# A new searched order, the first h earlier, and one last store in a two-layer decoder trunk

## The chip, the cores and the metric

The kernel runs on one core of one Trainium2 chip. The time is the device time of one execution in microseconds, and the figure compared is the median over several runs. Beside it there is one profiled execution, whose trace says what each engine did.

The engines have these names: PE is TensorE (matrix multiplies), PEld its weight loads, DVE is VectorE, ACT is ScalarE, POOL is GpSimd, and SP is SyncE, which in this kernel issues nearly all DMA transfers. A line number such as L126 is the line of the kernel that recorded an instruction.

## The reference

The program computes a hybrid decoder trunk of two layers on x (256 positions, width 2048) and a conditioning vector c (width 2048), all in float32:

```python
for layer in range(2):
    shift, scale, gate = split(silu(c) @ ada_w[layer] + ada_b[layer], 3)    # ada_w: 2048 x 6144
    h = x * (1.0 + scale) + shift
    if layer == 0:
        y = ssd_mixer(h, ...)        # h @ a_in_w (2048 x 10304), causal conv, state-space scan, gate, @ a_out_w (4096 x 2048)
    else:
        y = dilated_mixer(h, ...)    # h @ b_in_w (2048 x 4096), three dilated attention groups, gate, @ b_out_w (1024 x 2048)
    x = layer_norm(alpha * x + (1.0 + gate) * y, ln_g[layer], ln_b[layer])
    if layer == 0:
        k_sh, v_sh = shared_kv(x, kv_w)      # x @ kv_w (2048 x 6144)
return x
```

Most of the work is the large matrix products, each of whose weights is read from memory once, and the two `silu(c) @ ada_w` products, which read 50 MB each for a single vector.

## The kernel before, in words

**Products in two parts.** A float32 weight is split into a high part that TensorE takes at its fast rate and a low part that holds the rest. `load_piece` (L115) reads a weight piece `raw` of 128 x 1024 numbers (512 KB) with a DMA on the SP queue. `split` (L122) lets ACT copy it to `whi` (L126) and DVE subtract that from `raw` to get `wlo` (L127). There are 393 such splits. The activation h is split in the same way into a high part (`hhi`, in the traces `act`) and a low part (`hlo`). PE then makes three products, high by high, low by high and high by low, and adds them in one accumulator. L161 to L164 (`cm_piece`), L175 and L177 (`cm_part`) and L216 to L218 are these products. At the start the first four pieces are loaded and split in two halves each (128 x 512), and those halves are the first work of PE.

**The columns of ada_w.** `silu(c)` is spread over all partitions by `spread` (L516: PE makes the copy in an accumulator, ACT copies it to `cb__72`, L522). Then DVE multiplies a loaded block `araw` (128 x 2048, 1 MB) with it and sums along the row: L298 in `ada_dot`. One such dot gives 128 entries of shift, scale or gate. For the first two tiles of 128 entries the dot is cut in smaller pieces (L303), since h cannot be made without them.

**The first h.** The width of 2048 is 16 tiles of 128. `h_step` (L452) makes one of them. Its shift and scale are the sums of L308 and L309. For tile 0, ACT makes the high part in one step straight from x (L471), and DVE makes the plain product `htmp` (L472), from which the low part is subtracted later. For all the others ACT makes the plain product `htmp` (L468) and copies it to the high part (L469).

**What sets the order.** The program is written as one list of instructions. `arrange` (L1630) then searches an order: `forward` (L1330) simulates each engine with a table of durations and a model of DMA, and each trial moves some keys in a stretch of 100 us at random. ROUNDS trials are made, and the order with the smallest simulated end is the one that is built. In the model a DMA adds its bytes divided by RATE (425 GB/s) to the time at which DMA is free (L1392). Each engine runs its own list strictly in the order found, SP included, so that an instruction that waits holds up everything behind it on the same engine. Pairs in `PINS` (L613 to L623 for the start) fix the order of two instructions beforehand.

**The last store.** The output goes out in blocks. The last block of 128 rows is finished by `by_root` (L1104): a product on PE, a copy on ACT (L1107) and a store (L1108). Columns 1024 to 1536 are done in two halves of 256 columns, one stored on the ACT queue and the other on SP behind the store of L1123.

## Time and profile before

| what | value |
|---|---|
| runs | 1243.59, 1243.82, 1248.12 us, median 1243.82 |
| the profiled execution | 1245.2 us, span of its trace 1243.3 us |
| PE busy | 1229.1 us (99% of the span) |
| DVE busy | 1033.1 us (83%) |
| ACT busy | 702.9 us (57%) |
| DMA | 334.46 MB, mean 269 GB/s, up to 422 GB/s in a slice |
| weight splits (L126, L127) | 393 each |
| dots over a whole column block (L298) | 92, 2286 ns each |

A row of the grouped views and of the timeline is read so: start and length in us (in the timeline), engine, line, operation, output and inputs by the program's names, partitions x elements, and the count; in brackets stands the idle time of the engine just before, and what ended it. "PE acc L177 <- DVE wlo L127: 2.2, 3, 1.7" in the list of waits says that PE waited 2.2 us in all, 3 times, at most 1.7 us, for a low weight part of DVE. In the table by stretch an engine's entry is its busy time with the number of its instructions; behind POOL stand the granted clock of TensorE (1.00 is full speed), the busy share of the DMA engines and GB/s.

### The profile page before, as it was taken

The numbers are of one execution on the slowest core, as the hardware profiler recorded it, in microseconds if no ns is written. First come the engines' busy times: TensorE is split into PE (matmuls) and PEld (weight loads), VectorE is DVE, ScalarE is ACT, GpSimd is POOL, SyncE is SP. The second block draws the span as 40 slices with busy tenths as digits, with TensorE's granted clock in tenths as the row PEclk, the third lists the DMA queues.
The fourth block names the chain that finished last, engine by engine and source line by source line (L and its number), as shares of the span: only waits on it lengthen the run. The fifth ranks groups of instructions, "written<-read, shape, count | busy, mean of one in ns | idle before, by whom it ended". The sixth has DMA issues, their size and how long they took to land.

```text
span 1243.3 us, 18078 instructions
## 1 busy us (share of the span) xinstructions
PE 1229.1 (99%) x6712; PEld 1059.3 (85%) x6712; DVE 1033.1 (83%) x1480; ACT 702.9 (57%) x1055; POOL 0.2 (0%) x4
## 2 busy tenths in 40 slices
PE   8999999999999999999999999999999999999998
PEld 7989888888888888888888888888888888888886
DVE  5999998989999999968987698999945746757777
ACT  4645476668848589864345455444445644444561
POOL 0000000000000000000000000000000000000000
PEclk9999999999999999999999999999999999999999
DMA  9999977755786855648997679999965553452571
GB/s 368 421 422 422 422 266 236 249 200 193 265 311 236 308 195 192 240 159 321 395 390 258 234 249 370 393 393 400 374 226 184 196 186 116 158 192 75 192 282 68
DMA packets 81886, 334.46 MB, mean 269 GB/s; under 512 B 9124, under 2 KB 10116, under 8 KB 69640
## 3 DMA queue, kind: packets, MB, share of 16 engines
q1 hardware_dynamic: 81656, 333.20, 72.9%
q8 instruction: 52, 0.85, 0.3%
q14 instruction: 34, 0.28, 0.1%
q10 hardware_dynamic: 144, 0.13, 0.0%
HBM read 331.11 MB, written 2.18 MB: 268 GB/s over the span
## 4 chain that ended last, share of the span: by engine, by line
PE 91%; DMA 3%; DVE 3%; issue 1%; ACT 0%; SPq 0%; DVEq 0%
PE acc L175 24%; PE acc L216 13%; PE acc L217 13%; PE acc L218 13%; PE acc L177 13%; PE acc L163 2%; PE acc L161 2%; PE acc L164 2%; PE py L725 2%; DMA raw<-in_win 2%; DMA araw<-in_ada 2%; DVE wlo L127 1%; DVE araw L298 1%; PE po L1013 1%; PE aux L989 1%
## 5 line engine op out<-in xcount | busy, mean ns | idle before, releaser
L126 ACT ACTIVATE whi<-raw 128x1024 fp32r<-128x1024 f32 (+1 forms) x393 | 408.9, 1048 | 321.1 <-PE acc L175 130.9
L127 DVE TENSOR_TENSOR wlo<-raw,whi 128x1024 fp32r<-128x1024 f32 (+1 forms) x393 | 469.9, 1210 | 114.4 <-ACT whi L126 109.1
L175 PE MATMUL acc<-act,whi 128*128 128x512 f32 x1456 | 379.9, 395 | 0.6 <-DVE kk L198 0.6
L175 PEld LDWEIGHTS acc<-act,whi 128*128 128x128 f32 x1456 | 261.4, 188 | 46.3 <-issue 0.9
L217 PE MATMUL acc<-wlo,act 128*128 128x512 f32 x672 | 257.0, 394 | 0.0
L216 PE MATMUL acc<-whi,act 128*128 128x512 f32 x672 | 252.6, 396 | 0.1
L298 DVE SCALAR_TENSOR_TENSOR araw<-araw,cb__72 128x2048 f32<-128x2048 f32 x92 | 210.1, 2286 | 15.3 <-DMA araw<-in_ada 15.2
L177 PEld LDWEIGHTS acc<-act,wlo 128*128 128x128 f32 x1456 | 201.3, 190 | 17.6 <-DVE wlo L127 3.3
L177 PE MATMUL acc<-act,wlo 128*128 128x256 f32 x1456 | 213.2, 284 | 2.3 <-DVE wlo L127 2.2
L218 PE MATMUL acc<-whi,act 128*128 128x512 f32 x432 | 161.1, 393 | 0.0
L217 PEld LDWEIGHTS acc<-wlo,act 128*128 128x128 f32 x672 | 126.6, 188 | 26.1 <-issue 0.7
L216 PEld LDWEIGHTS acc<-whi,act 128*128 128x128 f32 x672 | 126.0, 188 | 26.0 <-issue 0.7
L218 PEld LDWEIGHTS acc<-whi,act 128*128 128x128 f32 x432 | 81.1, 188 | 16.6 <-issue 0.5
L218 PE MATMUL acc<-whi,ylo 128*128 128x512 f32 x240 | 89.8, 391 | 0.0
L163 PE MATMUL acc<-act,whi 128*128 128x256 f32 x208 | 52.3, 285 | 3.2 <-ACT act L469 2.1
L164 PE MATMUL acc<-act,wlo 128*128 128x256 f32 x208 | 52.8, 285 | 0.0
L218 PEld LDWEIGHTS acc<-whi,ylo 128*128 128x128 f32 x240 | 44.9, 188 | 9.2 <-DVE ylo L785 0.2
L163 PEld LDWEIGHTS acc<-act,whi 128*128 128x128 f32 x208 | 38.5, 192 | 4.5 <-ACT act L469 2.3
L161 PE MATMUL acc<-act,whi 128*128 128x256 f32 x208 | 42.1, 285 | 0.0
L683 ACT ACTIVATE seg<-cbc,cumT 128x128 f32<-128x128 f32 x128 | 40.1, 389 | 0.6 <-DMA cbc<-cumd 0.6
L164 PEld LDWEIGHTS acc<-act,wlo 128*128 128x128 f32 x208 | 38.8, 193 | 0.7
L383 DVE SCALAR_TENSOR_TENSOR cacc<-ct,prm,cacc 128x255 f32<-128x255 f32 (+2 forms) x84 | 37.0, 475 | 1.0 <-ACT cacc L380 0.8
(270 smaller groups left out, 1152.5 us busy)
## 6 DMA issues: line engine op xcount, KB each, us to landing
araw<-in_ada SPq DMA_DIRECT2D x92, 1024.0 KB, 7.5
raw<-in_win SPq DMA_DIRECT2D x86, 512.0 KB, 9.9
raw<-in_wsub SPq DMA_DIRECT2D x70, 512.0 KB, 4.2
raw<-in_wout SPq DMA_DIRECT2D x64, 512.0 KB, 5.4
raw<-in_wbin SPq DMA_DIRECT2D x64, 512.0 KB, 3.9
raw<-in_wkv SPq DMA_DIRECT2D x48, 512.0 KB, 4.3
raw<-in_wk SPq DMA_DIRECT2D x48, 512.0 KB, 6.8
cbc<-cumd SPq DMA_DIRECT2D x16, 512.0 KB, 5.3
```

Of the source, the lines that this page charges most:

```text
L126: S.activation(hi[:, c_], raw[:, c_], AF.Copy)
L127: m = V.tensor_tensor(lo[:, c_], raw[:, c_], hi[:, c_].bitcast(F32), op=ALU.subtract)
L161: T.matmul(o, hi[:, k, c_], alo[:, kt, :], start=False, stop=kt == k1 - 1, skip_group_check=True)
L163: note("product", T.matmul(o, hi[:, k, c_], ahi[:, kt, :], start=kt == k0 and n % 2 == 0, stop=False, skip_group_check=True))
L164: T.matmul(o, lo[:, k, c_], ahi[:, kt, :], start=False, stop=False, skip_group_check=True)
L175: T.matmul(ps[n], hi[:, k, c_], both[:, kt], start=first, stop=False, skip_group_check=True)
L177: T.matmul(ps[n][:, 0, :], lo[:, k, c_], high[:, kt, :], start=first, stop=False, skip_group_check=True)
L216: begin = T.matmul(ps[b], h_, hi[:, k, :], start=kt == k0, stop=False)
L217: T.matmul(ps[b], h_, lo[:, k, :], start=False, stop=False)
L218: end = T.matmul(ps[b], l_, hi[:, k, :], start=False, stop=kt == k1 - 1)
L298: V.scalar_tensor_tensor(raw, raw, 1.0, cb_, op0=ALU.mult, op1=ALU.mult, accum_out=to)
L683: m = S.activation(seg[:, hh, b, :], cbc[:, hh, b, :], AF.Relu, bias=cumT[:, b, h0 + hh:h0 + hh + 1], scale=-1.0)
```

## The change

It has three parts.

- **The first two h.** Tile 1 is now made like tile 0: its high part in one ACT step from x, and its plain product on DVE. New pins put the first high h behind the copy of the first half of the first weight piece and ahead of that of the second piece's first half, and the second high h behind the first piece's second half and ahead of the second piece's second half; the later copies of the spread c come behind the first high h.
- **The last store.** The two halves of columns 1024 to 1536 go out in one store of 256 KB on SP, behind the store of the last 512 columns.
- **The search.** In its model no DMA lands before 3.5 us (FIRST) plus its own time, and past 155 us (WAVE) it counts with 380 GB/s (LATE_RATE) in place of 425. It makes 260 trials in place of 520.

No matrix product, weight load or dot is added or taken away.

```diff
--- before.py
+++ after.py
@@ -123,10 +123,11 @@
 
         hi, lo = into or [wp.tile([P, 1024], F32R, name=n_, bufs=4) for n_ in ("whi", "wlo")]
         for c_ in parts(1024, n):
-            S.activation(hi[:, c_], raw[:, c_], AF.Copy)
+            a = S.activation(hi[:, c_], raw[:, c_], AF.Copy)
             m = V.tensor_tensor(lo[:, c_], raw[:, c_], hi[:, c_].bitcast(F32), op=ALU.subtract)
             if n > 1:
                 note("low", m)
+                note("high", a)
         return hi.rearrange("p (k n) -> p k n", k=2), lo.rearrange("p (k n) -> p k n", k=2)
 
     def stir(to, n, after=None):
@@ -464,12 +465,12 @@
                         if kt > 1:
                             ada_bias(0, slice(kt, kt + 1), slice(0, 2))
                         t = pe.tile([P, L], F32, name="htmp")
-                        if kt:
+                        if kt > 1:
                             S.activation(t, xts[kt // 2][:, kt % 2, :], AF.Identity, bias=shift(0, kt), scale=scale(0, kt))
                             S.activation(hhi[:, kt, :], t, AF.Copy)
                         else:
-                            S.activation(hhi[:, 0, :], xts[0][:, 0, :], AF.Identity, bias=shift(0, 0), scale=scale(0, 0))
-                            note(("dot", 0), V.tensor_scalar(t, xts[0][:, 0, :], scale(0, 0), shift(0, 0), op0=ALU.mult, op1=ALU.add))
+                            note("hhi", S.activation(hhi[:, kt, :], xts[0][:, kt, :], AF.Identity, bias=shift(0, kt), scale=scale(0, kt)))
+                            note(("dot", kt), V.tensor_scalar(t, xts[0][:, kt, :], scale(0, kt), shift(0, kt), op0=ALU.mult, op1=ALU.add))
                         late.append(lambda: note("hlo", V.tensor_tensor(hlo[:, kt, :], t, hhi[:, kt, :].bitcast(F32),
                                                                         op=ALU.subtract)))
 
@@ -519,7 +520,7 @@
                         m = T.matmul(pc[:, k * P:k * P + P], cs[:, 4 * i + k:4 * i + k + 1].to_broadcast([P, P]), ident,
                                      start=True, stop=True)
                     c_ = slice(512 * i + P * k0, 512 * i + P * k1)
-                    S.activation(cb_[:, c_], pc[:, P * k0:P * k1], AF.Copy)
+                    note("cb", S.activation(cb_[:, c_], pc[:, P * k0:P * k1], AF.Copy))
                     return m
 
                 for i in range(2):
@@ -620,6 +621,9 @@
                 line = dot[:2] + dot[3:5] + dot[2:3] + dot[5:] + low[0:4:2] + noted["hlo"][:1] + low[4:5] + dots[:2] + low[6:7] + dots[2:] + \
                     low[1:4:2] + noted["hlo"][1:2] + low[5::2]
                 PINS.extend(zip(line[1:], line))
+                high, hhis = noted["high"], noted["hhi"]
+                PINS.extend([(hhis[0], high[0]), (high[2], hhis[0]), (hhis[1], high[1]), (high[3], hhis[1])] +
+                            [(m, hhis[0]) for m in noted["cb"][3:]])
                 PINS.extend((m, noted["hlo"][4], 0) for m in noted["later"])
                 bc_conv(0, tiles(first[0]))
                 xs_conv(0, tiles(first[1]))
@@ -1101,26 +1105,28 @@
         PINS.append((first.ins.name, last.ins.name))
         T.matmul(po_, pick[:, k, :], rlo[:, c], start=False, stop=False)
 
-    def by_root(b, po_, c, by=nc.sync):
+    def by_root(b, po_, c):
 
         T.matmul(po_, diag[:, b], u[b][:, c], start=False, stop=True)
         S.activation(u[b][:, c], po_, AF.Copy)
-        return by.dma_start(out[b * P:b * P + P, c], u[b][:, c])
+        if not b or c.start < 1024:
+            nc.sync.dma_start(out[b * P:b * P + P, c], u[b][:, c])
 
     S.activation(diag[:, 0], ident, AF.Copy, scale=r0)
     by_root(0, *chunks[4])
     r, mean = ln_scale((1,), st8, False)
-    line, sent = newton[:], []
+    line = newton[:]
     S.activation(diag[:, 1], ident, AF.Copy, scale=r)
     for c in range(4):
         cs_ = slice(512 * c, 512 * c + 512)
         line.append(V.scalar_tensor_tensor(u[1][:, cs_], u[1][:, cs_], mean, lnt[:, 0, cs_], op0=ALU.subtract, op1=ALU.mult))
         if c < 3:
             for chunk in chunks[c:c + 1 + c // 2]:
-                sent.append(by_root(1, *chunk, nc.scalar if chunk is chunks[3] else nc.sync).ins.name)
+                by_root(1, *chunk)
             continue
         line.append(V.scalar_tensor_tensor(u[1][:, cs_], u[1][:, cs_], r, lnt[:, 1, cs_], op0=ALU.mult, op1=ALU.add))
-        PINS.append((sent[2], nc.sync.dma_start(out[P:, cs_], u[1][:, cs_]).ins.name, 0))
+        m = nc.sync.dma_start(out[P:, cs_], u[1][:, cs_])
+        PINS.append((nc.sync.dma_start(out[P:, 1024:1536], u[1][:, 1024:1536]).ins.name, m.ins.name, 0))
     PINS.extend((b.ins.name, a.ins.name) for a, b in zip(line, line[1:]))
 
 
@@ -1239,9 +1245,10 @@
 
 
 RATE, DMALAT, LANES = 425e3, 2.0, 8
-
-
-ROUNDS = 520
+FIRST, WAVE, LATE_RATE = 3.5, 155.0, 380e3
+
+
+ROUNDS = 260
 COLD = 6.2
 LOOK = 3
 
@@ -1389,7 +1396,7 @@
         start[i] = t
         if v.e == "SP":
             free["SP"] = t + v.occ
-            dmafree = max(dmafree, t + v.occ + DMALAT) + v.nb / RATE
+            dmafree = max(dmafree, t + v.occ + DMALAT, FIRST if t > 0.2 else 0.0) + v.nb / (RATE if t < WAVE else LATE_RATE)
             fin[i] = dmafree + v.lat
             lanes.append(fin[i])
         elif v.e is None:
```

Since the order is searched anew, instructions move on every engine. Three places are shown. The first is ACT's list from the first weight copies on. `raw_184`, `raw_187`, `raw_193` and `raw_214` are the first four weight pieces, in halves of 512 columns; `act0_85` is the high part of h, `htmp` its plain product, and `cb__72` the spread c. Before (one copy, `whi_238<-raw_184`, stands ahead of the first row):

```order
L126 ACTIVATE whi_274<-raw_187 128x512
L522 ACTIVATE cb__72<-acc_161 128x256
L126 ACTIVATE whi_301<-raw_193 128x512
L471 ACTIVATE act0_85<-xt_171,mod0_81 128x256
L126 ACTIVATE whi_333<-raw_214 128x512
L522 ACTIVATE cb__72<-acc_165 128x512
L126 ACTIVATE whi_238<-raw_184 128x512
L126 ACTIVATE whi_274<-raw_187 128x512
L126 ACTIVATE whi_301<-raw_193 128x512
L126 ACTIVATE whi_333<-raw_214 128x512
L468 ACTIVATE htmp_228<-xt_171,mod0_81 128x256
L469 ACTIVATE act0_85<-htmp_228 128x256
```

and now:

```order
L126 ACTIVATE whi_238<-raw_184 128x512
L472 ACTIVATE act0_85<-xt_171,mod0_81 128x256
L126 ACTIVATE whi_274<-raw_187 128x512
L126 ACTIVATE whi_301<-raw_193 128x512
L523 ACTIVATE cb__72<-acc_161 128x256
L126 ACTIVATE whi_333<-raw_214 128x512
L523 ACTIVATE cb__72<-acc_165 128x512
L126 ACTIVATE whi_238<-raw_184 128x512
L472 ACTIVATE act0_85<-xt_171,mod0_81 128x256
L126 ACTIVATE whi_274<-raw_187 128x512
L126 ACTIVATE whi_301<-raw_193 128x512
L126 ACTIVATE whi_333<-raw_214 128x512
```

The first high h moved ahead of two weight copies and a c copy, the second ahead of three weight copies, and the second is one step in place of two. DVE has a second `htmp` step in its list instead.

The second place is DVE's list in the middle of the first layer, at 324 to 341 us of the trace before. `araw_...` are column blocks with their dots (L298, now L299), `raw_...` weight pieces with their low parts (L127); the numbers rise in the order of the program's text. Before:

```order
L298 SCALAR_TENSOR_TENSOR araw_2405,mod0_81<-araw_2405,cb__72 128x2048
L298 SCALAR_TENSOR_TENSOR araw_2408,mod0_81<-araw_2408,cb__72 128x2048
L127 TENSOR_TENSOR wlo_3400<-raw_3397,whi_3399 128x1024
L127 TENSOR_TENSOR wlo_3422<-raw_3419,whi_3421 128x1024
L727 TENSOR_TENSOR y2_92<-y2_92,sz_2854 128x512
L383 SCALAR_TENSOR_TENSOR cacc_3323<-y5_95,prm_73,cacc_3323 128x255
L298 SCALAR_TENSOR_TENSOR araw_2455,mod0_81<-araw_2455,cb__72 128x2048
L127 TENSOR_TENSOR wlo_3452<-raw_3449,whi_3451 128x1024
L127 TENSOR_TENSOR wlo_3474<-raw_3471,whi_3473 128x1024
L298 SCALAR_TENSOR_TENSOR araw_2606,mod0_81<-araw_2606,cb__72 128x2048
```

and now:

```order
L299 SCALAR_TENSOR_TENSOR araw_2405,mod0_81<-araw_2405,cb__72 128x2048
L127 TENSOR_TENSOR wlo_3400<-raw_3397,whi_3399 128x1024
L127 TENSOR_TENSOR wlo_3422<-raw_3419,whi_3421 128x1024
L299 SCALAR_TENSOR_TENSOR araw_2408,mod0_81<-araw_2408,cb__72 128x2048
L127 TENSOR_TENSOR wlo_3452<-raw_3449,whi_3451 128x1024
L127 TENSOR_TENSOR wlo_3474<-raw_3471,whi_3473 128x1024
L299 SCALAR_TENSOR_TENSOR araw_2455,mod0_81<-araw_2455,cb__72 128x2048
L127 TENSOR_TENSOR wlo_3499<-raw_3496,whi_3498 128x1024
L127 TENSOR_TENSOR wlo_3521<-raw_3518,whi_3520 128x1024
```

The dot of `araw_2455` stood ahead of the low parts of `raw_3449` and `raw_3471` and now stands behind them; that of `araw_2408` moved behind two low parts as well.

The third place is DVE's list at 829 to 839 us of the trace before. `araw_7986`, `araw_8061`, `araw_8108`, `araw_8183` and `araw_8230` are successive columns of the second layer; L316 (now L317) adds a bias. Before:

```order
L127 TENSOR_TENSOR wlo_7967<-raw_7964,whi_7966 128x1024
L127 TENSOR_TENSOR wlo_7992<-raw_7989,whi_7991 128x1024
L298 SCALAR_TENSOR_TENSOR araw_8183,mod1_82<-araw_8183,cb__72 128x2048
L298 SCALAR_TENSOR_TENSOR araw_8230,mod1_82<-araw_8230,cb__72 128x2048
L127 TENSOR_TENSOR wlo_8014<-raw_8011,whi_8013 128x1024
L127 TENSOR_TENSOR wlo_8042<-raw_8039,whi_8041 128x1024
```

and now:

```order
L299 SCALAR_TENSOR_TENSOR araw_7986,mod1_82<-araw_7986,cb__72 128x2048
L127 TENSOR_TENSOR wlo_7967<-raw_7964,whi_7966 128x1024
L317 TENSOR_TENSOR mod1_82<-mod1_82,cc_74 128x16x2
L127 TENSOR_TENSOR wlo_7992<-raw_7989,whi_7991 128x1024
L299 SCALAR_TENSOR_TENSOR araw_8061,mod1_82<-araw_8061,cb__72 128x2048
L127 TENSOR_TENSOR wlo_8014<-raw_8011,whi_8013 128x1024
```

Up to the low part of `raw_8011` the dots of three columns fewer have been done. The last dot of this layer, of `araw_8864`, stood behind the low part of `raw_8532` and now stands behind that of `raw_8671`, six pieces later.

## The prediction, made before the changed kernel had run

> **What bounds the kernel now.** I read the page first, for the share of each engine and the chain that ended last.
>
> ```profile
> span 1243.3 us, 18078 instructions
> PE 1229.1 (99%) x6712; PEld 1059.3 (85%) x6712; DVE 1033.1 (83%) x1480; ACT 702.9 (57%) x1055; POOL 0.2 (0%) x4
> PE 91%; DMA 3%; DVE 3%; issue 1%; ACT 0%; SPq 0%; DVEq 0%
> ```
>
> PE is busy for 1229.1 of 1243.3 us and carries 91% of the chain. The change alters no matmul: it is worth at most what PE loses, by standing still or by running slowly. So the second view is the list of what PE waits for, the third the busy time by stretch (columns: length, PE, PEld, DVE and ACT busy, POOL, granted clock, DMA share, GB/s).
>
> ```profile
> PE acc L177 <- DVE wlo L127: 2.2, 3, 1.7
> PE acc L163 <- ACT act L469: 2.1, 1, 2.1
> ...
> 20.96:23.63 2.67, 0.61 (x6) 0.61 (x6) 1.31 (x4) 1.97 (x4) 0.00 (x0) 1.00 1.04 433
> 23.63:27.05 3.42, 3.42 (x16) 3.13 (x15) 1.00 (x2) 1.28 (x2) 0.00 (x0) 0.50 1.01 422
> ...
> 60.00:80.00 20.00, 20.00 (x125) 17.94 (x124) 18.52 (x21) 10.96 (x15) 0.00 (x0) 1.00 1.02 420
> ...
> 320.00:380.00 60.00, 58.07 (x321) 49.35 (x320) 55.22 (x72) 35.08 (x55) 0.00 (x0) 1.00 0.85 309
> ...
> 800.00:840.00 40.00, 39.09 (x222) 33.89 (x221) 38.84 (x45) 17.74 (x23) 0.00 (x0) 1.00 1.00 392
> ```
>
> The reader is to see four things. PE stood still around 21 us and then ran 3.42 us at half clock. From 60 to 80 us (the stretches from 40 to 160 read alike) PE never stops, but DMA is full too, at 420 GB/s. PE loses 60 - 58.07 = 1.93 us between 320 and 380 and 40 - 39.09 = 0.91 us between 800 and 840, both with DVE above 90% and DMA at 0.85 and 1.00.
>
> **The first h.** ACT rows, then DVE and PE rows, of the start:
>
> ```profile
> 10.58 1.32 ACT L126 ACTIVATE whi<-raw 128x512 fp32r<-128x512 f32 x2 [2.33 <-DMA raw<-in_win]
> 12.07 0.62 ACT L126 ACTIVATE whi<-raw 128x512 fp32r<-128x512 f32 x1
> 12.59 0.59 ACT L471 ACTIVATE act<-xt,mod 128x256 fp32r<-128x256 f32 x1
> 19.68 2.35 ACT L126 ACTIVATE whi<-raw 128x512 fp32r<-128x512 f32 x4 [4.42 <-DMA raw<-in_win]
> 21.94 0.58 ACT L468 ACTIVATE htmp<-xt,mod 128x256 f32<-128x256 f32 x1
> 22.55 0.42 ACT L469 ACTIVATE act<-htmp 128x256 fp32r<-128x256 f32 x1
> ...
> 11.12 0.16 DVE L309 TENSOR_TENSOR mod<-acc,mod 128x2 f32<-128x2 f32 x1
> 11.32 0.41 DVE L472 TENSOR_SCALAR htmp<-xt,mod 128x256 f32<-128x256 f32 x1
> ...
> 19.71 0.16 DVE L309 TENSOR_TENSOR mod<-acc,mod 128x2 f32<-128x2 f32 x1
> ...
> 10.81 1.33 PE L519 MATMUL acc<-cc 128*128 128x128 f32 x10
> 13.24 0.50 PE L163 MATMUL acc<-act,whi 128*128 128x256 f32 x2 [1.09 <-ACT act L471]
> 23.02 0.39 PE L163 MATMUL acc<-act,whi 128*128 128x256 f32 x1 [2.06 <-ACT act L469]
> ```
>
> The shift and scale of tile 0 are there at 11.12 + 0.16 = 11.28, but ACT reaches its h at 12.59, behind three weight copies and a c copy. Now h follows the first weight copy, which ends near 10.58 + 1.32 / 2 = 11.24. It starts at about 11.35 and ends at 11.35 + 0.59 = 11.94. PE is free at 10.81 + 1.33 = 12.14, so its wait of 1.09 goes. Queued behind the moved h on ACT are the copies of the second and third piece: one h later, at about 11.94 to 13.2. PE needs them only after the first piece's products, so I cost that at nothing; without that cover it is 0.59 us.
>
> **The second h.** Its mod is there at 19.71 + 0.16 = 19.87. Four weight copies (2.35) and two steps (0.58 and 0.42) stand before PE's restart at 23.02. Now one copy (2.35 / 4 = 0.59) ends at 20.27, one step of 0.59 at 20.86, and PE can restart at about 20.92, which is 2.1 us earlier. DVE takes over the plain product: one 128x256 instruction, 0.41 us as the row at 11.32 has it for the first h, between the second mod and the low parts. The low parts need ACT's copies, so it lies beside these. PE's work from 13.24 to 20.96 starts 1.1 us earlier, so about 20.92 - (20.96 - 1.1) = 1.1 us of standing still remain instead of 2.06.
>
> After the 2.06 us PE ran at a clock of 0.50 for 3.42 us: half of that, 1.7 us, is lost. The wait of 1.09 at 12.14 was followed by no such stretch. So I expect the remaining 1.1 us not to bring one, and the lead at 27 us is 2.1 + 1.7 = 3.8 us.
>
> **How much of that lead lasts to 160 us.** Three views of that stage: what ACT waits for from 40 to 160 us, then DVE's low parts and PE's first use of one.
>
> ```profile
> ACT whi L126 <- DMA raw<-in_win: 32.0, 28, 3.0
> ...
> 79.37 2.35 DVE L127 TENSOR_TENSOR wlo<-raw,whi 128x1024 fp32r<-128x1024 f32 x2
> ...
> 81.05 0.40 PE L217 MATMUL acc<-wlo,act 128*128 128x512 f32 x1
> ```
>
> Before 28 weight copies ACT waits for a landing, and DMA is full from the first microseconds: an earlier PE makes no byte land earlier. The first of the two low parts is done at 79.37 + 2.35 / 2 = 80.55 and used at 81.05: in this order PE can come 0.5 us earlier here and no more. The bounds are therefore 0.5 and 3.8 us. A new order can put ready products in front, and does move some weight loads ahead of a shift or scale column (1 MB, 2.5 us at 420 GB/s); the columns behind them come later in return. I take 1.8, a little below the middle of the bounds (2.15), since the 0.5 is a row and the 3.8 needs every landing to have slack.
>
> **The order between 320 and 380 us.** DVE, SP and PE rows:
>
> ```profile
> 326.19 2.29 DVE L298 SCALAR_TENSOR_TENSOR araw<-araw,cb__72 128x2048 f32<-128x2048 f32 x1
> 333.93 2.29 DVE L298 SCALAR_TENSOR_TENSOR araw<-araw,cb__72 128x2048 f32<-128x2048 f32 x1 [2.17 <-DMA araw<-in_ada]
> 336.14 2.35 DVE L127 TENSOR_TENSOR wlo<-raw,whi 128x1024 fp32r<-128x1024 f32 x2
> ...
> 326.30 2.54 SPq L277 DMA_DIRECT2D araw<-in_ada  x2
> ...
> 337.42 1.22 PE L177 MATMUL acc<-act,wlo 128*128 128x256 f32 x8 [1.73 <-DVE wlo L127]
> ```
>
> In the old order two column products (dots) follow each other, the next dot waits 2.17 us for the column issued at 326.30, and two low parts whose weights landed long before stand behind it; PE waits 1.73 us for the first. In the new order those two stand before that dot, right after the second one, so DVE does 2.35 us of work in the time that it stood still. I take the 1.73 whole. Its lower bound is nothing, if a later column stops PE instead; its upper the 1.93 that PE loses in this stretch.
>
> **The order between 800 and 840 us.**
>
> ```profile
> 834.22 2.29 DVE L298 SCALAR_TENSOR_TENSOR araw<-araw,cb__72 128x2048 f32<-128x2048 f32 x1 [0.37 <-DMA araw<-in_ada]
> 836.43 2.36 DVE L127 TENSOR_TENSOR wlo<-raw,whi 128x1024 fp32r<-128x1024 f32 x2
> ...
> 837.71 0.74 PE L177 MATMUL acc<-act,wlo 128*128 128x256 f32 x4 [0.33 <-DVE wlo L127]
> 839.27 0.69 PE L175 MATMUL acc<-act,whi 128*128 128x512 f32 x2 [0.58 <-DVE kk L198]
> ```
>
> Again two dots stand ahead of the low parts. In the new order three dots fewer have been done by there: 3 x 2.29 = 6.9 us of DVE and 3 MB of DMA move behind. Both PE waits, 0.33 + 0.58 = 0.91 us, should go. The dots come back later: the last one now follows six weight pieces more. What needs them, and its cover:
>
> ```profile
> 898.49 0.18 DVE L316 TENSOR_TENSOR mod<-mod,cc 128x16 f32<-128x16 f32 x1
> 952.95 0.42 DVE L242 TENSOR_TENSOR act<-htmp,act 128x256 fp32r<-128x256 f32 x1 [1.53 <-ACT act L241]
> ```
>
> The last bias is added at 898.49, and the next layer's h is split from 952.95 on: 54 us of cover for a delay of some 17 us (six pieces at about 2.9 us of PE), so I cost that at nothing. Without the cover it is those 17 us.
>
> Everywhere else the order is searched anew too, with half the trials. Outside these places I allow 0.5 us of new waits: between nothing and one more of the 1.73 kind.
>
> **The last store.** Issue rows, then two rows of the DMA list (KB each, median us to landing):
>
> ```profile
> 1238.71 0.38 ACTq L1108 DMA_DIRECT2D out<-u  x1
> 1238.98 0.41 SPq L1108 DMA_DIRECT2D out<-u  x1
> ...
> out<-u SPq DMA_DIRECT2D x7, 256.0 KB, 2.4
> out<-u ACTq DMA_DIRECT2D x1, 128.0 KB, 3.3
> ```
>
> The ACT store of 128 KB lands at 1238.71 + 3.3 = 1242.0 and the program ends 1.3 us behind. Now one store of 256 KB goes out where the last one did, at 1238.98, and waits for the same ACT copy as that one. At the 2.4 us of its kind it lands at 1241.4, 0.6 earlier; if it takes the 3.3, at 1242.3, 0.3 later. I take 0.3 earlier.
>
> **The sum.** 1.8 + 1.7 + 0.9 + 0.3 - 0.5 = 4.2 us off the profiled execution's 1245.2 us, which is 1241.0; the median of the runs is 1243.82, and the same 4.2 off that is 1239.6 us.
>
> **Rivals.** *All of it lasts.* The lead of 3.8 stays, and with 1.93, 0.91 and 0.6 that is 7.2 us: 1236.6 us. For it: PE works on several pieces at once and can reorder. Against it: the 0.5 us row.
>
> *The order gives nothing back.* PE finds other waits as long as the old ones, since every instruction between 160 and 1230 us may have moved, the model now takes 380 GB/s where the trace has 392 (800 to 840), and half the trials are made. Then 0.5 of the start and 0.3 of the store remain: 1243.0 us. Against it: the two moved places are plainly better.
>
> *Slower: the clock falls again and again.* If PE runs 2 to 4 us ahead of landings that cannot move, it stands still several times between 30 and 160 us. Each time that 2 us come together, as at 21 us, 3.42 us at half clock follow, 1.7 us that PE has no slack to win back. Then nothing of the start lasts, and the order's 1.7 + 0.9 + 0.3 - 0.5 = 2.4 stand against 1.7 each: from two such stretches on it is slower, and three give 1243.8 - 2.4 + 5.1 = 1246.5 us. Against it: the row of 320 to 380 us has a clock of 1.00 with 1.73 us of standing still in one wait.
>
> The Trainium skill ("TensorE: Matmul & The Clock Gate", Part 1) says that the clock halves after at least one idle window of about 3.4 us, and that the window runs freely. By that rule none of these waits is long enough, this rival could not happen, and the time would be the 1243.0 of the one before it. The trace disagrees, with 2.06 us ahead of the half clock, so the rival stays.
>
> **Chances and range.** Forecast 0.55, all lasts 0.17, nothing back 0.22, slower 0.06. About 0.5% (6.2 us) is what a measurement of this kernel can tell from no change. Faster by more needs nearly all of the second case and the edge of the first, 0.19; slower by more needs five half-clock stretches, 0.03; within it 0.78. Range 1236.6 (all lasts) to 1244.5 (nothing back and one or two new waits); the forecast's own is 1237.5 to 1241.5.
>
> **What would show it.** PE's first product with h at about 12.1 instead of 13.24 and its restart near 20.9 instead of 23.02; no stretch of 0.50 clock behind it; no wait of PE above 1 us between 320 and 380, none above 0.3 between 800 and 840; the lead at 160 us between 0.5 and 3.8; one 256 KB store last. I am wrong if PE shows new waits of together more than 2 us from 40 to 160 with the lead gone below 0.5, or if new waits beyond 160 us take back over 2 us.

## The result, and the profile after

The changed kernel takes 1240.41 us (median of 7 runs, 1239.74 to 1240.95), the kernel before in the same comparison 1244.48 us (1243.14 to 1248.12). The ratio is 0.9963, with an interval of 0.995 to 0.9975: 4.1 us or 0.37% less. The forecast was 1239.6 us. The sum came out, but most of its terms did not, and the experiments show that nearly the whole gain sits in two places of the order that the prediction had priced at 2.6 us together.

The page of the changed kernel, and what PE waits for in it:

```profile
span 1238.4 us, 18082 instructions
PE 1227.6 (99%) x6712; PEld 1058.1 (85%) x6712; DVE 1035.9 (84%) x1481; ACT 703.1 (57%) x1054; POOL 0.2 (0%) x4
...
PE acc L136 <- DVE magic L248: 1.0, 1, 1.0
PE acc L535 <- DMA y<-in_ada: 1.0, 2, 0.8
PE po L1110 <- DVE u L1122: 0.9, 1, 0.9
PE acc L535 <- DMA sz<-in_ada: 0.8, 1, 0.8
PE acc L217 <- ACT whi L126: 0.7, 2, 0.4
```

The waits for the first two h (2.1 and 1.1 us before) and for a low part (2.2 us) are gone from the list. To see when PE came ahead, count the matmuls that it has begun by a given time: the work is the same, so more of them by the same time is a lead. Stretches from 0, columns as in the prediction; kernel before:

```profile
0.00:27.00 27.00, 22.09 (x140) 20.72 (x141) 14.33 (x41) 10.99 (x20) 0.20 (x4) 0.94 0.95 361
0.00:160.00 160.00, 155.09 (x975) 141.42 (x976) 140.65 (x178) 84.45 (x116) 0.20 (x4) 0.99 1.00 410
0.00:320.00 320.00, 314.67 (x1871) 279.65 (x1872) 283.55 (x427) 205.61 (x321) 0.20 (x4) 0.99 0.83 316
0.00:380.00 380.00, 372.74 (x2190) 329.00 (x2191) 338.77 (x498) 240.69 (x375) 0.20 (x4) 1.00 0.83 315
0.00:800.00 800.00, 792.61 (x4328) 682.67 (x4329) 711.79 (x1050) 495.62 (x767) 0.20 (x4) 1.00 0.80 296
0.00:900.00 900.00, 891.70 (x4872) 768.40 (x4873) 808.39 (x1155) 538.78 (x821) 0.20 (x4) 1.00 0.82 306
```

and changed kernel:

```profile
0.00:27.00 27.00, 23.75 (x163) 21.75 (x164) 16.61 (x44) 12.97 (x23) 0.20 (x4) 1.00 0.95 361
0.00:160.00 160.00, 155.66 (x978) 139.87 (x978) 142.17 (x179) 84.57 (x114) 0.20 (x4) 1.00 1.01 411
0.00:320.00 320.00, 315.49 (x1873) 278.32 (x1874) 285.34 (x423) 203.79 (x314) 0.20 (x4) 1.00 0.83 316
0.00:380.00 380.00, 375.49 (x2209) 330.48 (x2210) 343.53 (x499) 243.79 (x378) 0.20 (x4) 1.00 0.84 317
0.00:800.00 800.00, 794.80 (x4341) 683.66 (x4342) 719.06 (x1059) 496.96 (x767) 0.20 (x4) 1.00 0.80 297
0.00:900.00 900.00, 894.80 (x4892) 770.91 (x4893) 807.37 (x1151) 541.33 (x822) 0.20 (x4) 1.00 0.82 305
```

The reader is to see the lead in matmuls: 23 at 27 us, 3 at 160, 2 at 320, then 19 at 380, 13 at 800, 20 at 900. The lead of the start is there and is gone again by 160 us. It is won a second time between 320 and 380 us, and a third part between 800 and 900.

The table gives the same lead in microseconds, for this kernel and for the experiments below. A matmul counts with the usual distance to the next one in the trace of before (0.227 us for 512 columns, 0.120 for 256, 0.109 for 128), summed over those begun by then, less the same sum of before.

| lead in us by | 27 | 160 | 320 | 380 | 720 | 800 | 900 |
|---|---|---|---|---|---|---|---|
| changed kernel | 3.2 | 0.4 | 0.5 | 3.5 | 2.8 | 2.7 | 4.5 |
| before, early h | 2.5 | 0.5 | 0.5 | 0.7 | 0.8 | -0.2 | -1.1 |
| changed, late h | 1.2 | 0.6 | 0.9 | 3.9 | 2.8 | 2.7 | 4.5 |
| before, one dot moved at 324 us | 1.1 | 0.2 | 0.2 | 3.2 | 2.8 | 1.6 | 0.9 |
| before, gate columns later | -0.4 | -0.1 | -0.2 | 0.5 | 0.6 | 0.5 | 2.3 |
| before, both of these | 1.4 | 0.5 | 0.2 | 3.5 | 3.0 | 3.0 | 4.8 |
| before, searched at 380 | 1.5 | 0.1 | 0.5 | 3.5 | 3.3 | 3.1 | 4.8 |
| changed, searched at 425 | 3.1 | 0.4 | 0.2 | 3.0 | 2.6 | 1.4 | 0.5 |

The start itself, in the changed kernel (ACT, DVE, then PE rows):

```profile
10.86 0.58 ACT L472 ACTIVATE act<-xt,mod 128x256 fp32r<-128x256 f32 x1
20.44 0.59 ACT L472 ACTIVATE act<-xt,mod 128x256 fp32r<-128x256 f32 x1
...
19.99 0.41 DVE L473 TENSOR_SCALAR htmp<-xt,mod 128x256 f32<-128x256 f32 x1
...
11.63 0.48 PE L164 MATMUL acc<-act,whi 128*128 128x256 f32 x2
21.08 0.50 PE L164 MATMUL acc<-act,whi 128*128 128x256 f32 x2
```

### The profile page after: what moved, and what is told of

Same layout as the page of the kernel before. It is cut to its first block, busy times and chain, and to the rows that moved or that the text cites. A ratio compares the mean times of both kernels' runs of the same rounds, so it can differ in the third digit from the quotient of the medians.

```text
span 1238.4 us, 18082 instructions
## 1 busy us (share of the span) xinstructions
PE 1227.6 (99%) x6712; PEld 1058.1 (85%) x6712; DVE 1035.9 (84%) x1481; ACT 703.1 (57%) x1054; POOL 0.2 (0%) x4
## 4 chain that ended last, share of the span: by engine, by line
PE 86%; DMA 11%; DVE 2%; ACT 1%; issue 0%; SPq 0%; ACTq 0%
PE acc L176 27%; PE acc L178 14%; PE acc L217 12%; PE acc L218 12%; PE acc L219 12%; DMA raw<-in_win 8%; DMA araw<-in_ada 2%; PE py L729 2%; PE aux L993 1%; PE aux L699 1%; PE po L1017 1%; PE po L1006 1%; PE aux L994 1%; PE aux L721 1%; DMA y<-in_ada 1%; PE aux L783 0%
## 5 line engine op out<-in xcount | busy, mean ns | idle before, releaser
L127 DVE TENSOR_TENSOR wlo<-raw,whi 128x1024 fp32r<-128x1024 f32 (+1 forms) x393 | 471.2, 1211 | 119.2 <-ACT whi L126 113.3
L299 DVE SCALAR_TENSOR_TENSOR araw<-araw,cb__72 128x2048 f32<-128x2048 f32 x92 | 210.3, 2285 | 7.0 <-DMA araw<-in_ada 6.7
```

The lines of the kernel that those rows point to most:

```text
L127: m = V.tensor_tensor(lo[:, c_], raw[:, c_], hi[:, c_].bitcast(F32), op=ALU.subtract)
L299: V.scalar_tensor_tensor(raw, raw, 1.0, cb_, op0=ALU.mult, op1=ALU.mult, accum_out=to)
```

## The experiments

Times are compared with runs of the kernel before on the same chip; its medians there were 1245.19, 1245.34 and 1245.51 us. In the first four, and in the two on the gate columns, the order that the search had found was kept, and single instructions were moved in it by hand:

```python
    def behind(e, what, place):                       # after the search, ahead of the loop that fixes the order
        (i, j), o = (made[(e, t)][n] for t, n in (what, place)), best[1]
        o.remove(i)
        o.insert(o.index(j) + 1, i)
```

### Is the lead of the start worth anything at the end?

Two theories. L: the landings between 40 and 160 us set PE's pace, and the lead melts. K: the lead is kept. First the kernel before with an early h, in ACT's list alone:

```diff
+    behind("Activation", ("act0_85", 0), ("whi_238", 0))
+    behind("Activation", ("htmp_228", 0), ("whi_238", 1))
+    behind("Activation", ("act0_85", 1), ("htmp_228", 0))
```

> The order of the kernel before, instruction for instruction, and in ACT's list alone the first high h moved ahead of two weight copies and a c copy, the second (still in two steps) ahead of three weight copies. Theory L (landings): between 40 and 160 us weights can't land earlier, so the lead that PE has at 27 us, some 3 us, melts to at most 0.6 us by 160 us, and the time is 0 to 0.6 us below the kernel before. Rival K (the lead is kept): the time is 2.5 to 3.8 us below. In both no stretch of half clock behind 21 us, if the standing still there stays below 1.2 us.

Measured: 1243.64 us (12 runs), ratio 0.9992, interval 0.9978 to 1.0006. The lead was 2.5 us at 27 and 0.5 us at 160, and no stretch of half clock came behind 21 us. The lead melted as L says. The ratio is 1.0 us less, more than the 0.6 of L, but the interval takes in no change at all; of K's range it leaves only the near edge.

Then the changed kernel with the late h of before:

```diff
+    behind("Activation", ("act0_85", 0), ("whi_301", 0))
+    behind("Activation", ("act0_85", 1), ("whi_333", 1))
```

> The changed kernel's order, and in ACT's list alone the first high h moved back behind three weight copies, and the second behind four. PE should wait for both again, about 1 and 2 us. Theory L (landings): the loss of 2.5 to 5 us at 27 us melts by 160 us, and the time is 0 to 0.6 us above the changed kernel. Rival K (the lead is kept): 2.0 to 4.5 us above it. If PE stands still for 2 us at one time, half a clock for some 3.4 us should follow, as in the kernel before; if it stands still for under 1.2 us, none.

Measured: 1240.25 us (6 runs, 1239.71 to 1241.73), against 1240.41 of the changed kernel; the ratios to the kernel before are 0.9959 and 0.9963. PE waits 3.1 us for the two h, and no cost of it shows at the end. Stretches of this kernel from 0:

```profile
PE acc L164 <- ACT act L472: 3.1, 2, 2.2
...
0.00:27.00 27.00, 21.68 (x148) 20.01 (x149) 15.15 (x43) 11.48 (x20) 0.20 (x4) 1.00 0.95 361
0.00:160.00 160.00, 154.29 (x979) 140.14 (x980) 142.21 (x179) 85.15 (x115) 0.20 (x4) 1.00 1.01 411
```

15 matmuls behind the changed kernel at 27 us (148 against 163), one ahead of it at 160 (979 against 978), with DMA full all the way. K has fallen. The expectation of half a clock behind a wait of 2 us has fallen too: 23.17 is the restart, and from 24 us on the clock is whole.

```profile
23.17 0.50 PE L164 MATMUL acc<-act,whi 128*128 128x256 f32 x2 [2.17 <-ACT act L472]
...
24.00:27.00 3.00, 3.00 (x22) 2.73 (x21) 0.84 (x3) 1.75 (x3) 0.00 (x0) 1.00 1.01 422
```

### The place at 324 to 341 us

```diff
+    behind("DVE", ("araw_2455", 0), ("wlo_3474", 0))
```

> The order of the kernel before, and in DVE's list alone one dot (the third of the place at 324 to 341 us) moved behind the two low parts that followed it. Theory O (the order of this place costs what PE loses there): the wait of 1.73 us goes and does not come back, 1.7 to 3.0 us below the kernel before (3.0 is the lead that the changed kernel wins between 320 and 380 us). Rival W (the wait moves): the dot ends 2.4 us later, so its buffer and the next column's load come 2.4 us later, weights queue behind that load, and PE waits elsewhere within the next 60 us: 0 to 0.7 us below.

Measured: 1243.72 us (12 runs, 1240.87 to 1246.36), ratio 0.9989, interval 0.9977 to 1.0001. In this place it did what theory O says, with one instruction of 18,000 moved. The stretch before, and with the dot moved:

```profile
320.00:380.00 60.00, 58.07 (x321) 49.35 (x320) 55.22 (x72) 35.08 (x55) 0.00 (x0) 1.00 0.85 309
```

```profile
320.00:380.00 60.00, 60.00 (x338) 52.01 (x337) 58.15 (x79) 37.40 (x59) 0.00 (x0) 1.00 0.87 324
```

17 matmuls more in the 60 us. The median is 1.5 us lower (1.4 by the ratio), between what O and W had said. The lead is 3.2 us at 380 and still 2.8 at 720, so the wait did not move on to the next weights: W has fallen. By the median alone it could not be told from nothing, because 1.9 us of the lead are lost again between 720 and 900 us, a place that this edit does not touch.

### The place at 829 to 839 us

```diff
+    behind("DVE", ("araw_8183", 0), ("wlo_8042", 0))
+    behind("DVE", ("araw_8230", 0), ("araw_8183", 0))
```

> The order of the kernel before, and in DVE's list alone the two dots of the place at 829 to 839 us moved behind the two low parts that followed them. Theory O: both waits of PE (0.33 and 0.58 us) go, 0.9 to 1.65 us below the kernel before (1.65 is the lead that the changed kernel wins between 800 and 840 us). Rival W (the wait moves): two column buffers come free 4.7 us later, the loads behind them too, and PE waits for a weight copy or low part within 30 us: 0 to 0.4 us below, or up to 1 us above.

Measured: 1247.21 us (12 runs, 1245.28 to 1252.53), ratio 1.0016, interval 1.0003 to 1.003: slower. Of the two waits named, that for the low part went, that for kk stayed, and a new one for a low part came within the next 60 us. Waits of PE from 800 to 900 us, then stretches:

```profile
PE acc L217 <- DVE wlo L127: 0.7, 1, 0.7
PE acc L175 <- DVE kk L198: 0.6, 1, 0.6
...
800.00:840.00 40.00, 39.37 (x225) 34.31 (x224) 38.82 (x44) 17.74 (x23) 0.00 (x0) 1.00 0.96 377
840.00:900.00 60.00, 59.33 (x322) 51.21 (x321) 57.10 (x62) 25.06 (x31) 0.00 (x0) 1.00 1.00 395
```

The wait moved, as W says, and the cost is above the 1 us that W allowed (2.0 us by the ratio, 0.4 to 3.7). Where the 2.0 us go the profile does not show: PE loses 1.30 us from 800 to 900 us, and 0.91, 1.57 and 1.44 in the profiles of before, of the early h and of the dot at 324 us, which leave this place as it was. The loads on SP kept their places, so with the dots delayed the two column buffers came free later. That this is why DMA falls to 377 GB/s before 840 us and is full again behind it fits, but was not tried apart.

### Too many columns ahead of 900 us?

The three profiles above with an edit in the kernel before (early h, 324 us, 829 us) and that of before itself hold the same order of this stretch (but for the two dots moved), and PE loses a different time in each. A stretch of 720 to 900 us, kernel before and before with the early h:

```profile
720.00:900.00 180.00, 179.09 (x972) 154.43 (x971) 170.49 (x190) 82.31 (x103) 0.00 (x0) 1.00 0.96 369
```

```profile
720.00:900.00 180.00, 177.67 (x962) 152.66 (x961) 168.36 (x185) 81.55 (x103) 0.00 (x0) 1.00 0.95 365
```

0.91 and 2.33 us; with the dot at 324 us moved it is 2.10. In before, DVE is busy for 95% and DMA for 96% of the stretch, so there is little slack; that each execution loses what its own transfers bring would fit, but was not shown. The next stretch has far less to do, and the changed kernel uses it. 900 to 960 us, before and changed:

```profile
900.00:960.00 60.00, 60.00 (x266) 49.60 (x265) 28.91 (x28) 28.54 (x35) 0.00 (x0) 1.00 0.62 212
```

```profile
900.00:960.00 60.00, 60.00 (x266) 49.57 (x266) 38.03 (x43) 32.13 (x43) 0.00 (x0) 1.00 0.71 242
```

So theory D: what helps is that columns go past 900 us. In the order of before, the 16 gate columns of the second layer (SP loads and DVE dots together) were put three places later (shortened, comments in place of the lines left out):

```diff
+    later("SP", ("raw_8611", "raw_8650", "raw_8689"))     # column k takes the place of k + 3; where the last three go
+    later("DVE", ("wlo_8596", "wlo_8635", "wlo_8674"))
+    # the load of the attention's bias goes behind raw_8789, the last addition behind the last dot
```

> The kernel before and its order, but the 16 gate columns of the second layer (1 MB load on SP and 2.29 us dot on DVE each, from about 820 us on) are three places later: each takes the place of the one that was three behind it, the last three follow 2, 4 and 6 weight pieces behind the old last one; the load of the attention's bias and the last addition go behind them. Theory D (the crowded stretch from 820 to 900 us is cleared when three columns, 3 MB and 6.9 us of DVE, go past it): PE's loss between 800 and 900 us falls from 0.9 to 2 us (three executions of this order) to under 0.4, the median to 1.0 to 2.0 us below the kernel before. Rival W (the wait moves to 900 to 960 us): PE loses there what it won, within 0.5 us of the kernel before. Rival S (another cause than the columns): the loss between 800 and 900 us stays above 0.9.

Measured: 1244.06 us (11 runs, 1242.24 to 1244.81) against 1245.51, ratio 0.9991, interval 0.9983 to 1.0.

```profile
800.00:840.00 40.00, 40.00 (x230) 35.09 (x229) 35.03 (x41) 18.23 (x24) 0.00 (x0) 1.00 0.92 344
840.00:900.00 60.00, 60.00 (x325) 52.00 (x325) 54.93 (x58) 26.11 (x31) 0.00 (x0) 1.00 0.99 389
900.00:960.00 60.00, 60.00 (x267) 49.60 (x266) 36.05 (x39) 29.16 (x37) 0.00 (x0) 1.00 0.66 233
```

PE loses nothing from 800 to 960 us, the lead grows by 1.8 us from 800 to 900 and stays. D holds in the place, and the median is 1.45 us lower as it said, though by the ratio it is 1.1 and the interval ends at no change; W and S have fallen. In the run on 829 us two dots were moved without their loads, and that won nothing. Then the same with the one dot at 324 us:

```diff
+    behind("DVE", ("araw_2455", 0), ("wlo_3474", 0))
```

> The same, and with it the one dot of 324 to 341 us moved behind two low parts as in the run on that place. Theories O and D together: 2.5 to 4.5 us below the kernel before, 1240.8 to 1242.8 us; what is left to the changed kernel then lies between 720 and 800 us and in the last store. If either gain is lost again on the way: less than 2 us below.

Measured: 1240.62 us (5 runs, 1240.38 to 1241.69), ratio 0.9966, interval 0.9952 to 0.9979. By the medians that is 4.9 us, a little more than expected. By the ratios the two edits gave 1.4 and 1.1 us alone and 4.2 together. Their intervals are too wide to say that this is more than the sum; the leads say why it can be, since the one dot's gain was lost again from 720 to 900 us as long as the gate columns stood in their old places. 4.2 us is the changed kernel's gain (0.9963), with 17 columns moved in the old order, the old start with its waits of 2.2 and 1.1 us, and the two last stores of before.

### Is it the rate in the model, or the draw?

Theory M: an order searched with 380 GB/s past 155 us holds, one searched with 425 does not. S: the draw of the random search decides.

```diff
-FIRST, WAVE, LATE_RATE = 3.5, 155.0, 380e3
+FIRST, WAVE, LATE_RATE = 3.5, 155.0, 425e3
```

> The changed kernel with one number altered, LATE_RATE 425e3 in place of 380e3: the order is searched with 425 GB/s throughout, everything else (first h, last store, 260 trials, the first landing) as changed. Theory M (the rate in the model makes the order robust): PE loses at least 1 us in the sum of the stretches 320 to 380, 720 to 800 and 800 to 900 us, the median is 1243 to 1247 us, and the runs lie over 3 us apart, as those of the kernel before do. Rival S (the draw of the search decides, not the rate): no such pattern, the median can be anywhere from 1239 to 1247 us, and a median below 1241.5 us speaks for it.

```diff
-    key, best, near = [float(v.i) for v in P[0]], None, random.Random(0)
+    key, best, near = [float(v.i) for v in P[0]], None, random.Random(1)
```

> The changed kernel with another seed of the search (1 in place of 0), LATE_RATE 380e3 as changed. Theory M: another order with the same property, median 1239.5 to 1242 us, runs within 2.5 us of each other, PE losing under 0.7 us in the sum of 320 to 380, 720 to 800 and 800 to 900 us. Rival S: the draw decides, a median above 1243 us or runs over 3 us apart speak for it.

Both edits together:

> The changed kernel with LATE_RATE 425e3 and seed 1. Theory M: 1243 to 1247 us and runs over 3 us apart, with losses of PE at 320 to 380 or 720 to 900 us. Rival S: a median below 1241.5 us.

In the kernel before:

```diff
+WAVE, LATE_RATE = 155.0, 380e3
-            dmafree = max(dmafree, t + v.occ + DMALAT) + v.nb / RATE
+            dmafree = max(dmafree, t + v.occ + DMALAT) + v.nb / (RATE if t < WAVE else LATE_RATE)
```

> The kernel before (old first h, two last stores, 520 trials, no first landing in the model) with one thing of the change: past 155 us the search counts with 380 GB/s. Theory M together with the finding that the start is worth nothing at the end: all of the gain but the 0.3 us of the store, 1240 to 1242 us, runs within 2.5 us of each other. Rival K (part of the gain needs the earlier h or the model's first landing): 1243 us or more. Rival S: anywhere.

And the changed kernel with a still lower rate, and with the old number of trials:

```diff
-FIRST, WAVE, LATE_RATE = 3.5, 155.0, 380e3
+FIRST, WAVE, LATE_RATE = 3.5, 155.0, 350e3
```

> The changed kernel with LATE_RATE 350e3 in place of 380e3. Theory M (the lower the rate in the model, the more columns go past the crowded stretch): at least three columns' dots behind 900 us, no loss of PE from 720 to 900 us, runs within 2.5 us, median 1239.5 to 1241 us, like the changed kernel or up to 1 us better. Rival (350 is too low, the search gives up order elsewhere for a shortage that is not there): 1241.5 us or more.

```diff
-ROUNDS = 260
+ROUNDS = 520
```

> The changed kernel with 520 trials of the search in place of 260. If the halved trials cost something: 0.3 to 1 us below the changed kernel, with the two remaining waits of PE near 712 and 160 us smaller. If not: within 0.3 us of it.

Measured, with PE's loss from 720 to 900 us in the profile (180 less PE's busy time) and the dots behind 900 us. The runs were made on different chips; the ratio, to the kernel before on the same chip, is what compares:

| order | median, us | runs, us | ratio (interval) | loss 720-900 | dots past 900 |
|---|---|---|---|---|---|
| before, 425 (loss: before, with early h, with the dot at 324 us moved) | 1245.34 | 1241.55 to 1250.18 (35) | 1 | 0.91, 2.33, 2.10 | 0 |
| changed, 425 | 1242.92 | 1240.68 to 1245.49 (12) | 0.9986 (0.9971 to 1.0) | 2.70 | 1 |
| changed, 425, seed 1 | 1241.31 | 1240.43 to 1243.66 (12) | 0.9974 (0.9961 to 0.9987) | 0 | 1 |
| before, 380 | 1241.44 | 1239.49 to 1243.82 (12) | 0.9964 (0.9951 to 0.9978) | 0 | 2 |
| changed, 380 | 1240.41 | 1239.74 to 1240.95 (7) | 0.9963 (0.995 to 0.9975) | 0 | 3 |
| changed, 380, seed 1 | 1240.68 | 1239.74 to 1242.61 (12) | 0.9963 (0.9951 to 0.9975) | 0 | 4 |
| changed, 380, 520 trials | 1242.23 | 1241.43 to 1243.57 (9) | 0.9976 (0.9966 to 0.9986) | 0 | 4 |
| changed, 350 | 1240.05 | 1239.62 to 1240.72 (5) | 0.9958 (0.9946 to 0.9971) | 0 | 5 |

Behind 900 us the dots' own busy time is 2.29 us in the order searched at 425, 6.89 in the changed one and 11.47 in that of 350:

```profile
900.00:960.00 60.00, 2.29 (x2) 1.00 0.65 226
```

```profile
900.00:960.00 60.00, 6.89 (x6) 1.00 0.71 242
```

```profile
900.00:960.00 60.00, 11.47 (x11) 1.00 0.80 289
```

The number of instructions is twice that of the dots, since each has a read of its accumulator. Where it is odd, the read of a dot that ended ahead of 900 us is counted too; some orders have a dot across the edge.

Against what was expected: the order at 425 lost PE time as M says, with a median just under M's range; seed 1 at 425 is S's case (1241.31 us, no loss). The order of before at 380 has the median that M gave it, but its runs lie 4.3 us apart where 2.5 was expected, and those of seed 1 at 380 2.9 us. The order at 350 did what M says. For 520 trials neither expectation holds.

What follows. The lower the rate in the model, the more columns go past the crowded stretch, as M says, and no order with two or more of them there lost anything from 720 to 900 us. The kernel before with the rate alone has nearly all of the gain, although its start keeps the late h. But the draw counts too: seed 1 at 425 lost nothing there either, with one column past 900 us and a stretch as full as the others, and seed 0 at 425 lost 2.70 us. 720 to 900 us, seed 0 and seed 1 at 425:

```profile
720.00:900.00 180.00, 177.30 (x961) 152.73 (x960) 166.19 (x184) 80.93 (x101) 0.00 (x0) 1.00 0.95 363
```

```profile
720.00:900.00 180.00, 180.00 (x978) 155.93 (x977) 168.50 (x185) 83.81 (x105) 0.00 (x0) 1.00 0.95 370
```

DVE is busy for 92% where PE loses and for 94% where it does not, DMA for 95% in both. So the busy shares do not tell by themselves whether an order loses. These are single profiles, and what spares seed 1 the loss stays open. 520 trials at 380 gave 1242.23 us, slower than 260 (by 1.8 us in the medians; the intervals of the ratios overlap). That kernel lacks 0.9 us of the lead at 900 us (3.6 against 4.5), and its last stage waits longer (1.7 in place of 0.9 us):

```profile
PE po L1110 <- DVE u L1122: 1.7, 1, 1.7
```

All of the newly searched orders, those at 425 too, are free of the loss at 320 to 380 us; so that one was the old draw's own. How the gain between 720 and 900 us splits between rate and draw is open with one to three orders for each. The kernel at 350 has the lowest median, 0.4 us below the changed one (0.6 by the ratios), which its interval does not tell from it.

## Why the prediction was right in its sum and wrong in its terms

**The start: 1.8 us taken, about 0.4 measured.** The rows were as forecast: first product with h at 11.63 (about 12.1 forecast), the restart at 21.08 (20.92), no half clock, a lead of 3.2 us at 27 (3.8). The failing step is "I take 1.8, a little below the middle of the bounds". Both bounds came from rows, but they were not alike: DMA at 1.00 to 1.02 and 413 to 423 GB/s in every stretch of before from 20 to 160 us says that the landings set the pace (in the first 10 us it was 0.79 and 269, so not from the first microseconds), and in the run with the late h a PE 2 us later at 27 us came out the same. The lower bound, 0.5 us, was the answer. With one resource full, nothing spoke for the middle of the two.

**The half clock.** That 2.06 us were followed by a half clock and "the wait of 1.09 at 12.14 was followed by no such stretch" was read as a rule on how long PE stands. Waits of 2.17 us (late h) and 2.47 us (the run on 324 us) were followed by a whole clock. And where it came, as in before, its 1.7 us were made up by 160 us with the rest: the early h had no half clock and was 0.5 us ahead there. The rival of repeated half clocks did not come true: no trace of this case has one between 29 and 1235 us.

**320 to 380 us: 1.73 taken, 3.0 measured.** The mechanism was right, and the run with one dot moved shows it alone. The size was read from the one named wait, and the bound of 1.93 from PE's busy time. Both miss gaps that are shorter than the modelled end of a matmul: by the matmuls begun, 321 against 338, some 3 us were at stake. From the start of one matmul to the next, 1.9 us are lost at the named wait, and most of the rest from 372 to 377 us, in gaps of 0.1 to 0.3 us.

**800 to 840 us: 0.9 taken, 1.65 measured between 800 and 840.** Here the reason given, that two dots stand ahead of two low parts, was not enough: moving just these won 0.8 us of lead by 840 us and lost 1.1 again by 900, and the kernel was slower. The other half of that passage, three columns going behind, was treated as a side cost to be covered by 54 us. It was the gain, as the gate columns' run shows (1.6 us of lead between 800 and 840), and covered it was.

**New waits: 0.5 taken, about 0.7 measured** between 380 and 800 us (the lead goes from 3.5 to 2.7). The largest is here, in the changed kernel:

```profile
711.00:714.00 3.00, 2.45 (x14) 1.79 (x13) 2.20 (x6) 1.85 (x3) 0.00 (x0) 1.00 0.63 214
```

**The last store: 0.3 taken.** From the last store's issue to the end of the span it was 1243.3 - 1238.98 = 4.3 us, and is now

```profile
1234.42 0.41 SPq L1129 DMA_DIRECT2D out<-u  x1
```

1238.4 - 1234.42 = 4.0 us. No run tries this part alone. In the other profiles with one last store it is 3.9 to 4.0 us (5.3 in one of six), in the others with two 4.0 to 4.6 (5.5 in one of six), so 0.3 is about the size, with single executions off by more than a microsecond. The sum by these sizes is 0.4 + 0.1 (160 to 320) + 3.0 - 0.7 + 1.8 (800 to 900) + 0.3, about 4.9 us, which is what the two profiled spans show (1243.3 - 1238.4). Errors of about 1.4 us too much (the start) and 2.2 us too little (the two places) hid each other: that 4.2 was forecast and the medians lie 4.1 apart is luck.

The rival "the order gives nothing back" spoke against the rate of 380, since the trace has 392 from 800 to 840 us. That was the wrong comparison: from 720 to 900 us the trace has 369, and the runs show that the orders searched with 380 and 350 lose nothing there. That a lower rate in the model leaves slack for what single transfers do is a reading of it, not shown.

## What to carry to other kernels

A lead that PE wins ahead of a stretch in which DMA is full can be worth nothing behind it, as here: test it by holding the start back in the fast kernel. In a static order, look for stretches in which PE loses time with DVE and DMA both near 95%, and for the slack stretch behind them, and try moving whole work items there, load and consumer together; here, moving the consumers alone only moved the wait. One profile of such an order shows one draw of its losses, so compare the distance of the runs too.

## What the runs showed of the hardware

**The spread belongs to the order, not to the chip.** On one chip the kernel before ran between 1242.69 and 1246.80 us (19 runs), the gate columns' order between 1242.24 and 1244.81 (11 runs) and the order at 350 between 1239.62 and 1240.72 (5 runs, and fewer runs spread less). The whole clock and the half one do not explain it: seven runs of the kernel before with a mean clock of 1.0 lay between 1243.33 and 1246.97 us on one chip.

**The half clock comes in pieces of one length on a fixed beat.** In before it was 23.63 to 27.05 us. In the run on 829 us it came twice:

```profile
7.89:11.31 3.42, 2.23 (x20) 2.09 (x20) 2.25 (x9) 0.08 (x1) 0.00 (x0) 1.00 1.02 390
11.31:14.72 3.41, 3.41 (x16) 3.26 (x16) 2.64 (x7) 2.46 (x5) 0.00 (x0) 0.50 1.04 416
...
21.55:24.96 3.41, 1.14 (x10) 0.94 (x9) 1.92 (x4) 2.61 (x5) 0.00 (x0) 1.00 1.02 423
24.96:28.37 3.41, 3.41 (x15) 3.12 (x14) 0.89 (x2) 1.46 (x2) 0.00 (x0) 0.50 1.01 411
```

The starts are 13.65 us apart, four times 3.41. In all fourteen traces of this case, from the first change of the clock that a trace records to the last, the time between two changes is a whole multiple of 3.41 us (from 1 to 362 of them). This agrees with what the Trainium skill says ("TensorE: Matmul & The Clock Gate", Part 1), that the window of about 3.4 us runs freely. That a whole window must be idle, as the Trainium skill says there too, does not agree: in before, PE worked 1.35 us of the 3.41 us ahead of the half clock.

Whether a wait of 2.1 to 2.5 us brings the half clock depends on where it falls in this beat. In before the whole 2.06 us lay in one window, and so did 2.27 us in the run above (21.55 to 24.96 us). With the late h, an edge of the beat cut the wait of 2.17 us, which left 1.10 and 1.06 us of standing still in the two windows, and the clock stayed whole:

```profile
18.70:22.11 3.41, 2.31 (x18) 1.98 (x17) 2.87 (x7) 1.98 (x4) 0.00 (x0) 1.00 1.06 417
22.11:25.52 3.41, 2.35 (x15) 2.16 (x16) 1.63 (x4) 1.39 (x3) 0.00 (x0) 1.00 1.00 418
```

Standing still is not all that counts, though. Ahead of the first half clock in the run on 829 us (11.31 us) PE stood still for only 1.19 us of the window and ran products of 64 and 128 columns for the rest, while 1.46 us in a window of the run on 324 us brought none. What exactly is counted stays open.
